# Table fetches, square sums and the programme of joins changed, and the gated convolution's strips set among attention's heads

## The chip, the cores and the metric

The kernel runs on one core of a Trainium2 chip. The metric is the device time of one execution in microseconds (us). The core has five engines that each run their own list of instructions in order and wait for one another at semaphores: TensorE (PE, matmuls), VectorE (DVE), ScalarE (ACT), GpSimd (POOL) and SyncE (SP, which here only starts transfers). Results of matmuls go to eight banks of PSUM.

## The reference

A trunk of two layers over T = 512 tokens with D = 1024 channels, all in float32. Each sub-layer is `x + rms_norm(f(rms_norm(x)))`. Layer 0 runs a gated short convolution and latent attention side by side; layer 1 a Conformer convolution; both end with a squared-ReLU MLP of 4096 hidden channels.

```python
def parallel_conv_mla(h, ...):
    proj = h @ w_in                       # 2208 columns
    gate_b, gate_c, xs, q_lat, kv_lat, k_rope = jnp.split(proj, cuts, axis=-1)
    y_a = gate_b * depthwise_conv(gate_c * xs, sc_kernel)      # width 3, 512 channels
    q = rms_norm(q_lat, q_norm) @ w_uq    # 8 heads of 64 + 32 (rope)
    kv = rms_norm(kv_lat, kv_norm) @ w_ukv
    ...
    y_b = block_attention(q_full, k_full, v)
    return jnp.concatenate([y_a, y_b], axis=-1) @ w_out

def conformer_conv(h, ...):
    a, g = jnp.split(h @ w_pw1 + b_pw1, 2, axis=-1)
    u = depthwise_conv(a * sigmoid(g), w_dw) + b_dw            # width 31
    return silu(layer_norm(u, ln_g, ln_b)) @ w_pw2 + b_pw2

def squared_relu_mlp(h, w1, w2):
    return jnp.square(jax.nn.relu(h @ w1)) @ w2
```

## The kernel before

Channels lie on the 128 partitions, tokens on the free axis; a tensor of 1024 channels is eight tiles of 128x512. Each operand of a matmul is split into a high and a low part, and a product is three matmuls: high by high, high by low, low by high (`mm`, L247 to L249). Weights come in strips of 128 output channels (128x1024 numbers): SP starts the transfer into a raw tile (L223), ACT copies it rounded into a high part (`whi`, L224), POOL subtracts for the low part (`wlo`, L225). There are two raw tiles (more in later phases) and eight slots each of `whi` and `wlo`. A whole strip against 512 tokens is 24 matmuls, against half the tokens 24 of half the length.

The order of the instructions on each engine is set by the framework's list scheduler, except in the programmes M0 to M3, where M2's vector instructions stand as written. The work in order:

- Phase m0. `split_x` loads each of eight x tiles, scales it (L572) and splits it; the rms-norm's factor R0 is not known yet, so it is applied to the results. ACT squares each tile (L359), DVE adds the squares (L334), PE sums over the channels (L369), a short chain on DVE makes the reciprocal root (L395 to L427), PE spreads it over the partitions (L434) and ACT copies it to R0 (L596).
- Five latent strips (`latent`, L604 multiplies by R0), the strip of the rope key, and the rope tables (L617 to L648: a transfer of the positions on ACT's queue, a chain on DVE and one Sin on ACT). The rope key's strip is multiplied by the table times R0 (L656).
- The gated convolution: `for i in range(4)`, three strips each (`win[6]` to `win[17]`), evicted by DVE with R0 (L672, L678, L695), the three taps on DVE, the two products on POOL (L679, L696). Its accumulators alternate between the PSUM banks S (three) and pj (two).
- V (four blocks, L715 to L727), then eight heads in the order of the table ATT: 'P' projects K (for two heads) and Q through pj banks, 'A' and 'B' attend for one half of the tokens: scores in S, maximum, exponential on ACT (L760), scaling (L763), transposes (L766) and the product with V in bank o.
- M0: the output projection wout for half A, `join` for A, wout for B. M2: a list of steps: up and down strips of the MLP's four groups, pw1 (two strips, Sigmoid, L801, product u, L805, and the start of a width-31 convolution on DVE), norm (LayerNorm and Silu, L863), pw2. A `join` or `norm` is a chain: sums of squares over channels, reciprocal root, spread, scale and split. While such a chain waits, `hold` and `pace` pull the steps that stand behind it in the list, if they belong to the other half of the tokens; what is pulled ends at the next step of the chain's own half. M3 is the last group.

A dummy activation is put ahead of a Sigmoid or Silu so that ACT loads its function table early: `nc.scalar.activation(warm[0], warm[0], AF.Sigmoid)` in `join` (L502) and the same with Silu in `layer_norm` (L848). `warm` is one tile, set once.

Of the kernel before, what the change touches and what calls it, by code (L numbers as in the profile page):

```python
# [132 lines left out]
def trunk(ctx: ExitStack, tc: tile.TileContext, a, out: bass.AP):  # L133
# [435 lines left out]
    def split_x(j):  # L569
        load_x(xs[j], j)  # L570
        t, (hi, lo) = scratch(T), (h.t[:, :T] for h in hs[j])
        nc.vector.tensor_scalar(out=t, in0=xs[j].t, scalar1=col(gains(0, 0) + j), scalar2=None, op0=ALU.mult)  # L572
# [96 lines left out]
    for i in range(4):  # L669
        accc = linear(strip(a["win"][6 + 3 * i]), hs)  # L670
        tcg = tmp("pr")[:, :T]
        nc.vector.tensor_tensor(out=tcg, in0=accc, in1=R0, op=ALU.mult)  # L672
        accx = linear(strip(a["win"][7 + 3 * i]), hs)
        cx = tmp("pr")
        nc.gpsimd.memset(cx[:, 0:1], 0.0)
        nc.gpsimd.memset(cx[:, T + 1 : T + 2], 0.0)
        tx = tmp("tq")
        nc.vector.tensor_tensor(out=tx, in0=accx, in1=R0, op=ALU.mult)  # L678
        nc.gpsimd.tensor_tensor(out=cx[:, 1 : T + 1], in0=tx, in1=tcg, op=ALU.mult)  # L679
        v = tmp("pr")[:, :T]  # L680
        nc.vector.tensor_scalar(
            out=v, in0=cx[:, 0:T], scalar1=col(V_SC + i * 3), scalar2=None, op0=ALU.mult
        )
        for k in (1, 2):
            nc.vector.scalar_tensor_tensor(
                out=v,
                in0=cx[:, k : k + T],
                scalar=col(V_SC + i * 3 + k),
                in1=v,
                op0=ALU.mult,  # L690
                op1=ALU.add,
            )
        accb = linear(strip(a["win"][8 + 3 * i]), hs)
        tb = tmp("pr")[:, :T]
        nc.vector.tensor_tensor(out=tb, in0=accb, in1=R0, op=ALU.mult)  # L695
        nc.gpsimd.tensor_tensor(out=v, in0=v, in1=tb, op=ALU.mult)  # L696
# [141 lines left out]
    def layer_norm(seg):  # L838
# [9 lines left out]
        nc.scalar.activation(warm[0], warm[0], AF.Silu)  # L848
# [300 lines left out]
```

## Time and profile before

| | us |
|---|---|
| median of three runs | 1176.1 (1175.84 to 1176.19) |
| the profiled execution | 1176.2 |
| its span | 1174.4 |
| PE busy | 1135.2 (97%) |
| POOL busy | 846.6 (72%) |
| ACT busy | 667.8 (57%) |
| DVE busy | 648.6 (55%) |

The span is the time from the first to the last instruction in the trace; 1.8 us lie around it. The mean granted clock of PE is 0.991. In a row of the profile stand start and duration, engine, line, operation, the tile written, the tiles read, the shape, and, in brackets, how long the engine was idle before it and on what it waited. S, pj, o and mi are PSUM banks, h the split input, hid the MLP's hidden tiles, ycat temporaries of phase m0, m and x the two streams of activations, pr the probabilities and pt their transposes, s small columns.

### The profile page before, as it was taken

Reading aid. Unit: us, or ns where it says so; the run is one execution under the profiler, and the core shown is the slowest. Engines: PE = TensorE matmul, PEld = TensorE weight load, DVE = VectorE, ACT = ScalarE, POOL = GpSimd, SP = SyncE. Lnnn points to the kernel's source line nnn. Section 1 sums busy time; section 2 is a strip of 40 time slices with the busy share of each in tenths; the row PEclk is TensorE's granted clock in tenths of the full one; section 3 lists DMA queues with packets and bytes.
Section 4 is the critical chain, followed back from the end, with each engine's and each line's share of the span. In section 5 each row is a group of like instructions: output and inputs, shape, how many; then the busy total and the mean of one; then the engine's idle time right before and its main releaser. Section 6 shows DMA issues by size and latency. Waiting matters only on the chain.

```text
span 1174.4 us, 22870 instructions
## 1 busy us (share of the span) xinstructions
PE 1135.2 (97%) x8850; PEld 1096.5 (93%) x8850; DVE 648.6 (55%) x1701; ACT 667.8 (57%) x1220; POOL 846.6 (72%) x409
## 2 busy tenths in 40 slices
PE   6999989999999999999999999999999999999995
PEld 4888879999999999899999999899999999999995
DVE  5652699554522124599965265699975272322123
ACT  7521667556845457545566678546467685545352
POOL 4664553148988888688886878698888877877681
PEclk9999999999999999999999999999999999999998
DMA  6421332037655555455554655455555555653431
GB/s 193 157 89 36 97 108 72 1 105 240 200 180 190 188 173 189 135 201 184 179 195 147 200 178 184 139 200 197 197 177 183 179 172 170 197 180 127 156 130 39
DMA packets 55405, 184.00 MB, mean 157 GB/s; under 512 B 6400, under 2 KB 10880, under 8 KB 55296
## 3 DMA queue, kind: packets, MB, share of 16 engines
q1 hardware_dynamic: 54720, 181.86, 46.8%
q8 instruction: 69, 1.13, 0.4%
q10 hardware_dynamic: 576, 0.68, 0.2%
q14 instruction: 40, 0.33, 0.1%
HBM read 180.42 MB, written 2.10 MB: 155 GB/s over the span
## 4 chain that ended last, share of the span: by engine, by line
PE 86%; ACT 4%; DVE 4%; POOL 2%; DMA 2%; issue 1%; POOLq 0%; ACTq 0%; DVEq 0%
PE S L247 22%; PE S L248 21%; PE S L249 21%; PE pj L247 6%; PE pj L248 6%; PE pj L249 6%; POOL wlo L225 2%; DMA raw<-in_w 1%; ACT whi L224 1%; DVE pr L763 1%; PE mi L369 1%; PE mi L434 1%; PE mi L766 1%; PE o L248 1%; DVE s L757 1%
## 5 line engine op out<-in xcount | busy, mean ns | idle before, releaser
L225 POOL TENSOR_TENSOR wlo<-raw,whi 128x1024 fp32r<-128x1024 f32 (+2 forms) x347 | 803.5, 2330 | 258.2 <-ACT whi L224 249.6
L224 ACT ACTIVATE whi<-raw 128x1024 fp32r<-128x1024 f32 (+2 forms) x347 | 355.9, 1031 | 378.0 <-PE S L248 173.1
L247 PE MATMUL S<-h,whi 128*128 128x256 f32 (+3 forms) x1208 | 347.3, 290 | 5.5 <-ACT h L231 3.7
L248 PE MATMUL S<-h,whi 128*128 128x256 f32 (+3 forms) x1208 | 348.4, 289 | 0.0
L249 PE MATMUL S<-h,wlo 128*128 128x256 f32 (+3 forms) x1208 | 348.3, 289 | 0.0
L247 PEld LDWEIGHTS S<-h,whi 128*128 128x128 f32 x1208 | 227.8, 190 | 10.8 <-ACT h L231 4.3
L247 PE MATMUL S<-hid,whi 128*128 128x256 f32 (+2 forms) x824 | 230.3, 282 | 2.3 <-DVE acc L334 1.8
L249 PEld LDWEIGHTS S<-h,wlo 128*128 128x128 f32 x1208 | 229.1, 190 | 3.5
L248 PEld LDWEIGHTS S<-h,whi 128*128 128x128 f32 x1208 | 228.9, 190 | 3.5 <-issue 0.2
L248 PE MATMUL S<-hid,whi 128*128 128x256 f32 (+2 forms) x824 | 230.9, 281 | 0.0
L249 PE MATMUL S<-hid,wlo 128*128 128x256 f32 (+2 forms) x824 | 230.4, 281 | 0.0
L828 DVE SCALAR_TENSOR_TENSOR pj<-u,taps,pj 128x240 f32<-128x240 f32 (+1 forms) x464 | 190.9, 483 | 1.0
L247 PEld LDWEIGHTS S<-hid,whi 128*128 128x128 f32 x824 | 154.8, 189 | 3.3 <-DVE acc L334 2.2
L249 PEld LDWEIGHTS S<-hid,wlo 128*128 128x128 f32 x824 | 155.6, 189 | 0.0
L248 PEld LDWEIGHTS S<-hid,whi 128*128 128x128 f32 x824 | 155.5, 189 | 0.1
L247 PE MATMUL pj<-h,whi 128*128 128x272 f32 (+3 forms) x344 | 105.8, 308 | 11.9 <-ACT h L231 10.2
L248 PE MATMUL pj<-h,whi 128*128 128x272 f32 (+3 forms) x344 | 105.1, 306 | 0.5 <-DVE h L234 0.5
L249 PE MATMUL pj<-h,wlo 128*128 128x272 f32 (+3 forms) x344 | 104.5, 304 | 0.0
L247 PEld LDWEIGHTS pj<-h,whi 128*128 128x128 f32 x344 | 64.9, 189 | 15.7 <-ACT h L231 11.0
L237 DVE TENSOR_TENSOR hid<-S,hid 128x256 fp32r<-128x256 f32 (+2 forms) x102 | 42.8, 420 | 54.3 <-ACT hid L231 54.0
L248 PEld LDWEIGHTS pj<-h,whi 128*128 128x128 f32 x344 | 65.0, 189 | 4.2 <-DVE h L234 1.8
L249 PEld LDWEIGHTS pj<-h,wlo 128*128 128x128 f32 x344 | 65.0, 189 | 2.6
(250 smaller groups left out, 1661.7 us busy)
## 6 DMA issues: line engine op xcount, KB each, us to landing
raw<-in_w SPq DMA_DIRECT2D x256, 512.0 KB, 3.3
raw<-in_pw SPq DMA_DIRECT2D x48, 512.0 KB, 3.4
raw<-in_win SPq DMA_DIRECT2D x16, 512.0 KB, 3.3
x<-in_xT SPq DMA_DIRECT2D x16, 256.0 KB, 4.6
raw<-in_wout SPq DMA_DIRECT2D x8, 512.0 KB, 3.3
raw<-in_wq SPq DMA_DIRECT2D x8, 192.0 KB, 2.3
...
```

The lines of the kernel that those rows point to most:

```text
L224: nc.scalar.activation(h, r, AF.Copy)
L225: nc.gpsimd.tensor_tensor(out=lo[:, c0:c1], in0=r, in1=h.bitcast(F32), op=ALU.subtract)
L237: eng.tensor_tensor(out=lo, in0=src, in1=hi.bitcast(F32), op=ALU.subtract)
L247: nc.tensor.matmul(acc, sh, mh, start=i == 0, stop=False)
L248: nc.tensor.matmul(acc, sh, ml, start=False, stop=False)
L249: nc.tensor.matmul(acc, sl, mh, start=False, stop=i == n - 1)
L369: nc.tensor.matmul(s[:, b : b + 1], q[:, sl.start - self.seg.lo : sl.stop - self.seg.lo], one, start=i == 0, stop=i == len(self.parts) - 1,)
L434: nc.tensor.matmul(o[:, sl], r[:, b : b + 1].to_broadcast([bw, P]), ident[:bw, :bw], start=True, stop=True,)
L757: nc.vector.reduce_max(out=mx, in_=S, axis=AX.X)
L763: eng.tensor_scalar(out=pr_, in0=pr_, scalar1=sm, scalar2=None, op0=ALU.mult)
L766: nc.tensor.transpose(tp[:, kb * P : (kb + 1) * P], pr_[:, kb * P : (kb + 1) * P], ident)
L828: nc.vector.scalar_tensor_tensor(out=dst, in0=src, scalar=wk, in1=acc, op0=ALU.mult, op1=ALU.add)
```

## The change

Five edits.

1. `split_x` squares x four tiles later (LAG); the last four squares come after all x tiles.
2. The dummy activations read a tile of the moment instead of `warm`: the Sigmoid's the squares' sum, the Silu's the negative mean. Each writes a small new tile.
3. In M2 the first group of pw1's steps is preceded by four down strips instead of two, for A and for B.
4. The gated convolution is a generator of pieces: three per group, and each piece computes one strip in a pj bank. The three pieces of the first group run where the loop stood; the other nine are taken one after every second entry of ATT. Temporaries come from ycat (16 tiles); the halo columns and their zeroing are gone, the outer taps work on 511 columns.
5. The tables TE and TO, V, Q and K's table lie in halves of weight-strip slots (`wtiles`) instead of slots of h, since h is read until the last gated strip.

```diff
-M2 = [... ('down', 'B', 0, 0, 0, 2), ('pw1', 'A', 0, 8), ('down', 'B', 0, 0, 2, 8), ... ('down', 'A', 1, 0, 0, 2), ('pw1', 'B', 0, 8), ('down', 'A', 1, 0, 2, 8), ...]
+M2 = [... ('down', 'B', 0, 0, 0, 4), ('pw1', 'A', 0, 8), ('down', 'B', 0, 0, 4, 8), ... ('down', 'A', 1, 0, 0, 4), ('pw1', 'B', 0, 8), ('down', 'A', 1, 0, 4, 8), ...]
+LAG = 4
+    def table():
+        return new(sp, "table", 2, 1)
...
         bc = rstds(ssq)
-        nc.scalar.activation(warm[0], warm[0], AF.Sigmoid)
+        nc.scalar.activation(table(), ssq.parts[0][:, :1], AF.Sigmoid)
...
         split((hi, lo), t, nc.vector, late=late)
-        s0.square(xs[j].t)
+        if j >= LAG:
+            s0.square(xs[j - LAG].t)
...
+    for j in range(NC - LAG, NC):
+        s0.square(xs[j].t)
+        settle()
...
-    for i in range(4):
-        accc = linear(strip(a["win"][6 + 3 * i]), hs)
...
+    def gated(i):
+        def part(n):
+            acc = linear(strip(a["win"][6 + 3 * i + n]), hs, acc=ps("pj"))
+            t = tmp("ycat")
+            nc.vector.tensor_tensor(out=t, in0=acc, in1=R0, op=ALU.mult)
+            return t
+
+        tcg = part(0)
+        yield
+        tx, cx, v = part(1), tmp("ycat"), tmp("ycat")
+        nc.gpsimd.tensor_tensor(out=cx, in0=tx, in1=tcg, op=ALU.mult)
+        w = [col(V_SC + i * 3 + k) for k in range(3)]
+        nc.vector.tensor_scalar(out=v, in0=cx, scalar1=w[1], scalar2=None, op0=ALU.mult)
+        for k, dst, src in ((0, v[:, 1:T], cx[:, : T - 1]), (2, v[:, : T - 1], cx[:, 1:T])):
             nc.vector.scalar_tensor_tensor(
+                out=dst, in0=src, scalar=w[k], in1=dst, op0=ALU.mult, op1=ALU.add
             )
+        yield
+        nc.gpsimd.tensor_tensor(out=v, in0=v, in1=part(2), op=ALU.mult)
         h = ypair()
         split((h[0].t, h[1].t), v, nc.gpsimd)
         ya.append(h)
+        yield
+
+    pieces = (i for n in range(4) for i in gated(n))
+    for _ in range(3):
+        next(pieces)
...
-    TE, TO = ht(), ht()
+    def wtiles(tag, dt=F32R):
+        t = new(wp, tag, N_W, STRIP, dt)
+        return t[:, :T], t[:, T:]
+
+    TE, TO = wtiles("wlo", F32)
...
-        h = ht(F32R), ht(F32R)
-        split(h, acc, nc.vector, rkv_c[:, b : b + 1])
-        V.append(h)
-    Qs = [(ht(F32R), ht(F32R)) for _ in range(2)]
+        if b % 2 == 0:
+            pair = tuple(zip(wtiles("whi"), wtiles("wlo")))
+        split(pair[b % 2], acc, nc.vector, rkv_c[:, b : b + 1])
+        V.append(pair[b % 2])
+    Qs = list(zip(wtiles("whi"), wtiles("wlo")))
...
-            tkns[p] = ht()
+            if p % 2 == 0:
+                tkns[p], tkns[p + 1] = wtiles("whi", F32)
...
-    for h, half in ATT:
+    for n, (h, half) in enumerate(ATT):
         if half == "P":
             project(h)
         else:
             attend(h, A if half == "A" else B)
+        if n % 2:
+            next(pieces, None)
...
-        nc.scalar.activation(warm[0], warm[0], AF.Silu)
+        nc.scalar.activation(table(), mu[:, :1], AF.Silu)
```

The new lines shift those that follow: a line of the kernel before has a number 1 to 15 higher in the changed one. The lists below name a tile by its kind and a running number.

The first place is the start of ACT's list. Before, with L502 and L848 the dummy activations of `warm`, L359 the squares, L231 the high part of an x tile (h):

```order
L562 ACT_TABLE_LOAD
L562 ACTIVATE s_75<-s_75 128x1
L502 ACT_TABLE_LOAD
L502 ACTIVATE warm_2837<-warm_2837 128x1
L848 ACT_TABLE_LOAD
L848 ACTIVATE warm_2837<-warm_2837 128x1
L502 ACT_TABLE_LOAD
L502 ACTIVATE warm_2837<-warm_2837 128x1
L848 ACT_TABLE_LOAD
L848 ACTIVATE warm_2837<-warm_2837 128x1
L359 ACTIVATE ycat_107<-x_79 128x512
L224 ACTIVATE whi_110<-raw_109 128x128
```

and now, with L360 the squares and L232 the high parts:

```order
L567 ACT_TABLE_LOAD
L567 ACTIVATE s_75<-s_75 128x1
L360 ACTIVATE ycat_151<-x_79 128x512
L225 ACTIVATE whi_108<-raw_107 128x128
L232 ACTIVATE h_87<-mi_104 128x512
L225 ACTIVATE whi_108<-raw_107 128x896
L225 ACTIVATE whi_122<-raw_121 128x256 x2
L232 ACTIVATE h_89<-o_117 128x512
L225 ACTIVATE whi_122<-raw_121 128x256 x2
L232 ACTIVATE h_91<-mi_137 128x512
L232 ACTIVATE h_93<-o_142 128x512
L232 ACTIVATE h_95<-mi_147 128x512
```

Four table loads with their dummies are gone from the start, and the squares but one stand further back.

The second place lies between the latents and attention. On PE before, pj_456 is the rope key's strip, S_519 the first gated strip, pj_552 and S_593 the next two, mi_481 the sums for the latents' norm:

```order
L249 MATMUL S_519<-h_101,wlo_515 128x512
L369 MATMUL mi_481<-kst,ycat_365 128x1 x4
L247 MATMUL pj_552<-h_87,whi_547 128x512
L248 MATMUL pj_552<-h_88,whi_547 128x512
...
L249 MATMUL pj_552<-h_101,wlo_548 128x512
L247 MATMUL S_593<-h_87,whi_588 128x512
```

and now, where S_646 is the first block of V and pj_519 the first gated strip:

```order
L250 MATMUL pj_519<-h_101,wlo_515 128x512
L248 MATMUL S_646<-whi_641,m_367 128x512
L248 MATMUL S_657<-whi_641,m_367 128x512
L248 MATMUL S_666<-whi_641,m_367 128x512
L370 MATMUL mi_481<-kst,ycat_365 128x1 x4
L248 MATMUL pj_552<-h_87,whi_547 128x512
L249 MATMUL pj_552<-h_88,whi_547 128x512
L250 MATMUL pj_552<-h_87,wlo_548 128x512
```

All gated strips are in pj banks now, so that pj_552 takes the bank of pj_456, and V's matmuls begin among them. On POOL at this place before, wlo_548 belongs to the second gated strip, and one gated strip follows upon another:

```order
L225 TENSOR_TENSOR wlo_548<-raw_546,whi_547 128x1024
L225 TENSOR_TENSOR wlo_589<-raw_587,whi_588 128x1024
L225 TENSOR_TENSOR wlo_627<-raw_625,whi_626 128x1024
L225 TENSOR_TENSOR wlo_660<-raw_658,whi_659 128x1024
L225 TENSOR_TENSOR wlo_701<-raw_699,whi_700 128x1024
L225 TENSOR_TENSOR wlo_739<-raw_737,whi_738 128x1024
```

and now, where L689 and L697 are the convolution's two products, wlo_642 is V's strip and L238 a low part of the convolution's result:

```order
L226 TENSOR_TENSOR wlo_548<-raw_546,whi_547 128x1024
L226 TENSOR_TENSOR wlo_587<-raw_585,whi_586 128x1024
L689 TENSOR_TENSOR ycat_579<-ycat_577,ycat_544 128x512
L697 TENSOR_TENSOR ycat_580<-ycat_580,ycat_616 128x512
L226 TENSOR_TENSOR wlo_642<-raw_640,whi_641 128x1024
L238 TENSOR_TENSOR ycat_620<-ycat_580,ycat_619 128x512
```

V's low part stands behind both products of the first group.

The third place is the join of half A at the end of layer 0 (after `('down', 'A', 0, 3, 0, 8)`), on PE. Before, S_5694 is a down strip of the other half, mi_5669 the spread of the reciprocal root, and S_5749, S_5826 and S_5851 are the first strips that read the join's h:

```order
L247 MATMUL S_5694<-hid_5258,whi_5511 128x256
L248 MATMUL S_5694<-hid_5259,whi_5511 128x256
L249 MATMUL S_5694<-hid_5258,wlo_5512 128x256
L434 MATMUL mi_5669<-kst,s_5623 128x128 x2
L247 MATMUL S_5749<-h_2181,whi_5547 128x256
L247 MATMUL S_5826<-h_2181,whi_5638 128x256
```

and now, where S_5720 is one more strip of the other half, mi_5650 the spread, and S_5795 to S_5897 the strips that read h:

```order
L248 MATMUL S_5676<-hid_5239,whi_5492 128x256
L249 MATMUL S_5676<-hid_5240,whi_5492 128x256
L250 MATMUL S_5676<-hid_5239,wlo_5493 128x256
L248 MATMUL S_5720<-hid_5225,whi_5528 128x256
...
L249 MATMUL S_5720<-hid_5240,whi_5528 128x256
L250 MATMUL S_5720<-hid_5239,wlo_5529 128x256
L435 MATMUL mi_5650<-kst,s_5604 128x128 x2
L248 MATMUL S_5795<-h_2164,whi_5619 128x256
L248 MATMUL S_5872<-h_2164,whi_5715 128x256
L248 MATMUL S_5897<-h_2164,whi_5752 128x256
```

A whole strip, S_5720, has come between the last part of the strips before and the spread.

More of the change, by code (lines that the diff above doesn't have):

```diff
@@ L35 @@
 M1 = []
-M2 = [('up', 'A', 0, 0, 0, 8), ('join', 'B', 0, 1), ('down', 'A', 0, 0, 0, 8), ('up', 'A', 0, 1, 0, 8), ('down', 'A', 0, 1, 0, 8), ('up', 'A', 0, 2, 0, 8), ('down', 'A', 0, 2, 0, 8), ('up', 'A', 0, 3, 0, 8), ('down', 'A', 0, 3, 0, 8), ('join', 'A', 0, 3), ('up', 'B', 0, 0, 0, 8), ('down', 'B', 0, 0, 0, 2), ('pw1', 'A', 0, 8), ('down', 'B', 0, 0, 2, 8), ('up', 'B', 0, 1, 0, 8), ('down', 'B', 0, 1, 0, 8), ('up', 'B', 0, 2, 0, 2), ('norm', 'A'), ('up', 'B', 0, 2, 2, 8), ('down', 'B', 0, 2, 0, 8), ('pw2', 'A', 0, 8), ('join', 'A', 1, 1), ('up', 'B', 0, 3, 0, 8), ('down', 'B', 0, 3, 0, 8), ('join', 'B', 0, 3), ('up', 'A', 1, 0, 0, 8), ('down', 'A', 1, 0, 0, 2), ('pw1', 'B', 0, 8), ('down', 'A', 1, 0, 2, 8), ('up', 'A', 1, 1, 0, 8), ('down', 'A', 1, 1, 0, 8), ('up', 'A', 1, 2, 0, 6), ('norm', 'B'), ('up', 'A', 1, 2, 6, 8), ('down', 'A', 1, 2, 0, 8), ('up', 'A', 1, 3, 0, 4), ('pw2', 'B', 0, 8), ('join', 'B', 1, 1), ('up', 'A', 1, 3, 4, 8), ('down', 'A', 1, 3, 0, 8), ('up', 'B', 1, 0, 0, 8), ('down', 'B', 1, 0, 0, 6), ('finish', 'A'), ('down', 'B', 1, 0, 6, 8), ('up', 'B', 1, 1, 0, 8), ('down', 'B', 1, 1, 0, 8), ('up', 'B', 1, 2, 0, 8), ('down', 'B', 1, 2, 0, 8)]
+M2 = [('up', 'A', 0, 0, 0, 8), ('join', 'B', 0, 1), ('down', 'A', 0, 0, 0, 8), ('up', 'A', 0, 1, 0, 8), ('down', 'A', 0, 1, 0, 8), ('up', 'A', 0, 2, 0, 8), ('down', 'A', 0, 2, 0, 8), ('up', 'A', 0, 3, 0, 8), ('down', 'A', 0, 3, 0, 8), ('join', 'A', 0, 3), ('up', 'B', 0, 0, 0, 8), ('down', 'B', 0, 0, 0, 4), ('pw1', 'A', 0, 8), ('down', 'B', 0, 0, 4, 8), ('up', 'B', 0, 1, 0, 8), ('down', 'B', 0, 1, 0, 8), ('up', 'B', 0, 2, 0, 2), ('norm', 'A'), ('up', 'B', 0, 2, 2, 8), ('down', 'B', 0, 2, 0, 8), ('pw2', 'A', 0, 8), ('join', 'A', 1, 1), ('up', 'B', 0, 3, 0, 8), ('down', 'B', 0, 3, 0, 8), ('join', 'B', 0, 3), ('up', 'A', 1, 0, 0, 8), ('down', 'A', 1, 0, 0, 4), ('pw1', 'B', 0, 8), ('down', 'A', 1, 0, 4, 8), ('up', 'A', 1, 1, 0, 8), ('down', 'A', 1, 1, 0, 8), ('up', 'A', 1, 2, 0, 6), ('norm', 'B'), ('up', 'A', 1, 2, 6, 8), ('down', 'A', 1, 2, 0, 8), ('up', 'A', 1, 3, 0, 4), ('pw2', 'B', 0, 8), ('join', 'B', 1, 1), ('up', 'A', 1, 3, 4, 8), ('down', 'A', 1, 3, 0, 8), ('up', 'B', 1, 0, 0, 8), ('down', 'B', 1, 0, 0, 6), ('finish', 'A'), ('down', 'B', 1, 0, 6, 8), ('up', 'B', 1, 1, 0, 8), ('down', 'B', 1, 1, 0, 8), ('up', 'B', 1, 2, 0, 8), ('down', 'B', 1, 2, 0, 8)]
@@ L668, in trunk @@
     ya = []
-    for i in range(4):
-        accc = linear(strip(a["win"][6 + 3 * i]), hs)
[L671 to L684, printed above, removed]
-            nc.vector.scalar_tensor_tensor(
[L686 to L691, printed above, removed]
-            )
[L693 to L696, printed above, removed]
+    def gated(i):
[11 more added lines that the diff above has]
+        for k, dst, src in ((0, v[:, 1:T], cx[:, : T - 1]), (2, v[:, : T - 1], cx[:, 1:T])):
+            nc.vector.scalar_tensor_tensor(
+                out=dst, in0=src, scalar=w[k], in1=dst, op0=ALU.mult, op1=ALU.add
+            )
+        yield
+        nc.gpsimd.tensor_tensor(out=v, in0=v, in1=part(2), op=ALU.mult)
         h = ypair()
@@ L878, in start @@
                 convolve(*todo.pop(0))
-    hid, sums, kept, us, lack, warm = {}, {}, {}, [], {}, []
+    hid, sums, kept, us, lack = {}, {}, {}, [], {}
     def seg_of(h, layer):
@@ L1033, in trunk @@
     us.extend(tmp("u") for _ in range(NC))
-    warm.append(new(sp, "warm", 1, 1))
-    nc.vector.memset(warm[0], 0.0)
     vs = [m.t for m in ms]
```

## The prediction

> **What bounds the kernel now.** I read the head of the page first, then a table of stretches, then the waits of TensorE (PE).
>
> ```profile
> PE 1135.2 (97%) x8850; PEld 1096.5 (93%) x8850; DVE 648.6 (55%) x1701; ACT 667.8 (57%) x1220; POOL 846.6 (72%) x409
> ```
>
> PE is busy in 97% of the span of 1174.4 us. The arithmetic on PE is the same in both kernels, so only the other 39 us can change, and the time in which PE is busy at a lower clock. Around the span lie 1.8 us (the profiled execution took 1176.2 us; the median of the runs shown is 1176.1, so what is summed against the one holds for the other). The stretches below give PE's busy time first, then weight loads, VectorE (DVE), ScalarE (ACT), GpSimd (POOL), and the granted clock:
>
> ```profile
> 10.00:20.00 10.00, 8.62 (x26) 4.91 (x25) 9.28 (x15) 9.15 (x18) 6.54 (x6) 1.00 0.61 203
> 60.00:120.00 60.00, 60.00 (x267) 48.82 (x266) 24.29 (x40) 11.79 (x18) 31.40 (x29) 1.00 0.19 59
> 140.00:150.00 10.00, 8.74 (x50) 7.21 (x49) 9.32 (x24) 9.02 (x20) 7.85 (x5) 1.00 0.45 147
> 150.00:160.00 10.00, 7.95 (x41) 6.68 (x40) 9.93 (x16) 5.78 (x12) 7.86 (x5) 0.83 0.29 92
> 170.00:180.00 10.00, 8.84 (x55) 7.24 (x54) 9.72 (x25) 8.37 (x20) 6.18 (x5) 1.00 0.20 63
> 470.00:480.00 10.00, 8.10 (x66) 7.65 (x65) 4.83 (x20) 6.32 (x14) 6.24 (x3) 1.00 0.43 147
> 480.00:490.00 10.00, 10.00 (x72) 9.96 (x73) 5.20 (x14) 3.55 (x8) 2.75 (x3) 0.83 0.32 107
> 740.00:750.00 10.00, 9.58 (x69) 9.58 (x70) 5.72 (x15) 3.07 (x9) 2.80 (x2) 0.83 0.32 107
> ```
>
> While the gated convolution runs (60 to 120) PE is full and DVE has 24.29 of 60 us of work. In attention (140 to 180) it is the other way round: DVE 9.3 to 9.9 of 10 us, PE 8.74, 7.95, 8.84. The rows of 150, 480 and 740 show a clock of 0.83. Half the clock for 3.4 of the 10 us gives that mean, and costs 1.7 us of work. The PE waits that go with it:
>
> ```profile
> PE S L247 <- ACT h L231: 3.7, 3, 1.7
> PE o L248 <- DVE s L758: 2.6, 3, 1.3
> PE mi L434 <- DVE s L420: 2.0, 2, 1.1
> PE mi L766 <- DVE pt L237: 1.8, 1, 1.8
> PE S L247 <- DVE u L805: 0.9, 1, 0.9
> PE S L247 <- ACT y L801: 0.4, 1, 0.4
> ```
>
> The joins (L434, then h L231), the Sigmoid (u L805, y L801) and attention (L758, pt L237) are the places. The start is a tenth part:
>
> ```profile
> 0.73 1.28 ACT L562 ACT_TABLE_LOAD   x1 [0.73 <-PEq L1137]
> ...
> 3.93 0.75 DVE L572 TENSOR_SCALAR mi<-x,vec 128x512 f32<-128x512 f32 x1 [3.04 <-DMA x<-in_xT]
> 4.96 3.80 SPq L208 DMA_DIRECT2D x<-in_xT  x6
> 6.79 1.28 ACT L848 ACT_TABLE_LOAD   x1
> 8.20 0.61 ACT L359 ACTIVATE ycat<-x 128x512 f32<-128x512 f32 x1
> 8.91 0.57 ACT L231 ACTIVATE h<-mi 128x512 fp32r<-128x512 f32 x1
> 9.52 0.69 DVE L234 TENSOR_TENSOR h<-mi,h 128x512 fp32r<-128x512 f32 x1 [4.83 <-ACT h L231]
> 9.54 0.79 PE L247 MATMUL pj<-h,whi 128*128 128x512 f32 x1 [9.54 <-ACT h L231]
> ```
>
> Five table loads of 1.28 us with a dummy activation each (first and last shown) hold ACT until 8.20, though DVE scaled the first x at 3.93. PE starts at 9.54, and between 10 and 20 it is idle for another 1.38 us.
>
> **The change, part by part.** Terms are after less before, in us.
>
> *Table fetches and squares.* Four of the five loads leave the start, so ACT can run the first square when x0 is there (3.93). By the rows 8.20 to 9.54, the square, the first weight piece and h take 1.34 us from ACT's start to PE's; counted from 3.93 with a little waiting for the weights that puts the first matmul near 5.5, 4 us earlier. It can't all be kept. The six later x's are issued at 4.96, and a transfer of x takes 4.6:
>
> ```profile
> x<-in_xT SPq DMA_DIRECT2D x16, 256.0 KB, 4.6
> ```
>
> They come from about 9.6 on, and DVE spends 0.75 (L572) and 0.69 (L234) on each, so the last is not split before 9.6 + 6 x 1.44 = 18.2. The squares' adds (0.69 each) now stand behind, which helps there. Before, PE's idle time up to 20 sums to 9.54 + 1.38 = 10.9; some 3.8 of it goes. Ends: -5 (all of the earlier start and the idle time after it) and -2 (PE merely waits later for x and the third strip). The other table loads move from the start to the joins' and norms' waits. Each is 1.28 and has 3 us of spreading and DVE work beside it there: nothing, as long as that chain is the longer.
>
> *Stalls ahead of attention.* Twelve gated strips filled PE between the latents and attention. Three are left there, and all use the two pj banks alone. So what they covered comes out. The rows:
>
> ```profile
> 35.11 0.58 ACT L596 ACTIVATE R<-mi 128x512 f32<-128x512 f32 x1
> 55.89 1.06 ACT L224 ACTIVATE whi<-raw 128x1024 fp32r<-128x1024 f32 x1 [1.91 <-DMA raw<-in_win]
> 56.86 0.67 ACT L634 ACTIVATE ycat<-o,kst 128x512 f32<-128x512 f32 x1
> 57.08 0.48 PE L247 MATMUL pj<-h,whi 128*128 128x512 f32 x1
> 59.02 0.68 DVE L672 TENSOR_TENSOR pr<-S,R 128x512 f32<-128x512 f32 x1
> 61.05 0.69 DVE L656 TENSOR_TENSOR ycat<-pj,ycat 128x512 f32<-128x512 f32 x1
> 71.98 1.29 POOL L696 TENSOR_TENSOR pr<-pr,pr 128x512 f32<-128x512 f32 x1 [3.98 <-DVE pr L695]
> 73.23 2.40 POOL L225 TENSOR_TENSOR wlo<-raw,whi 128x1024 fp32r<-128x1024 f32 x1
> 118.76 1.95 PE L434 MATMUL mi<-kst,s 128*128 128x128 f32 x16
> ```
>
> (a) R0: its spread now stands one strip (24 matmuls of 0.23) later on PE, and the next strip needs the bank that the first L604 empties: after the spread come 0.58 (L596) and one multiply by R0 (0.69, as L656), about 1.4 of wait with the semaphores; two weight copies (1.06 each) stand ahead of L596 on ACT now, so up to 2.6. (b) The second gated strip needs the bank of the rope key's strip (pj_456), which the multiply L656 empties, at the end of the rope chain. Before, that strip used S and only the multiply was late, at 61.05 to 61.74, with no PE wait. PE gets there at about 54.8 now (its 57.1 of before, less 3.7 from the start, plus 1.4 from a). The chain loses the weight copy ahead of its Sin (55.89, then L634 at 56.86: 1.3 with its wait) and L672 (0.68), and starts perhaps 0.4 earlier: 61.7 - 2.4 = 59.3, so 4.5 of wait. Ends: 2 (squeezed together by an emptier DVE) and 6.9 (chain where it was). (c) V's weights: their lo part stands on POOL behind the convolution's product (L696). After the last gated matmul come an eviction 0.69, the product 1.29 and the subtraction 2.40, against two spreads of 8 matmuls on PE (the last row's 16, 1.7 of its 1.95 before the next can start): 2.7. (d) The first head: K and Q must be evicted and split before the first score, and the strip that should cover this has its hi copy on ACT behind Q's:
>
> ```profile
> 130.52 0.62 ACT L231 ACTIVATE h<-tq 128x512 fp32r<-128x512 f32 x1
> ...
> 137.22 1.06 ACT L224 ACTIVATE whi<-raw 128x1024 fp32r<-128x1024 f32 x1 [2.21 <-DMA raw<-in_wout]
> ```
>
> Eviction 0.68 and Q's hi 0.62 are 1.3 before the first scores; then a whole hi copy (1.05) and the lo subtraction: 3.3 together. Ends 1 and 4. Sum of a to d 11.9; PE lost about 1.5 in the same part before, so +10.4 (ends +6 and +13).
>
> *The clock.* The dips at 156, 480 and 740 follow upon 1.8 us of idle PE (for pt) or two waits of about 1 close together (0.9 + 1.0 at the joins); 60 to 120, without idle time, has none. So b makes one (1.7), and c or d likely another: +2.7 (ends +1.7, +5). Here a rule of the Trainium skill differs. Its page "TensorE: Matmul & The Clock Gate", section "Why this matters for your kernels", asks for gaps of more than about 3 us before the rate halves. By it b alone would dip, this term would be 1.7, and the joins' dips below would not be for the change to remove. The trace speaks against it: two gaps of about 1 us were enough at 480.
>
> *Attention.* The nine other strips (24 x 0.23 = 5.5 us each, 50 together) now stand between heads. They bring DVE 9 evictions of 0.69 and three convolutions' taps (about 2 each): 12 us of work in 50 us of time. So DVE no longer bounds heads 0 to 5. Before, PE's idle time in the three stretches is 1.26 + 2.05 + 1.16 = 4.5, the dip 1.7, and small delays perhaps 2; heads 6 and 7 still run without cover, where some 1.8 stays: -6.4 (ends -3 and -9). TE, V, Q and K lie in weight slots now, which leaves three or four of eight to strips: from a slot's release to its use pass a transfer (no longer than x's 4.6), the hi copy (1.06) and the lo (2.40), 8.1 in all, against 11 us of two strips alone: hidden. Five of wout's eight strips, not all, are ready when attention ends. The other three need 2.40 on POOL each against 2 x 2.8 of PE per strip: nothing.
>
> *Joins.* Four down strips instead of two can be pulled into a join's waits. At join A one more (24 matmuls of 0.118 = 2.8) stands on PE between the column sums L369 and the spread L434; at join B 3.7 more, and 15 matmuls (1.8) behind the spread before the first h.
>
> ```profile
> 478.13 0.71 PE L434 MATMUL mi<-kst,s 128*128 128x128 f32 x4 [0.91 <-DVE s L420]
> 479.84 0.62 PE L247 MATMUL S<-h,whi 128*128 128x256 f32 x3 [1.00 <-ACT h L231]
> 629.96 1.28 ACT L863 ACT_TABLE_LOAD   x1
> 631.26 0.56 ACT L863 ACTIVATE pj<-m,vec 128x240 f32<-128x240 f32 x1
> 638.05 0.38 PE L247 MATMUL S<-h,whi 128*128 128x240 f32 x1 [1.70 <-ACT h L231]
> ```
>
> The chain on DVE ends at 478.1 in the first row, so the wait 0.91 goes, the wait 1.00 for h stays, and with one gap left the dip (1.7) goes: -2.7. Join B: waits 1.1 and 1.0 and the dip: -3.8. The Sigmoid's fetch is moved from the first glu's path: its two waits 0.9 and 0.4 go: -1.3. Norms: the Silu fetch (1.28) leaves the path between L860 and the first Silu, but strips that covered the norm have been used up earlier, and pw2 stands right behind the spread. Norm A's chain is eight Silu (0.56), each with a split on ACT, and the weight copies among them (1.05): some 10 us, and PE has 7 to 8 us of pw2's first three strips beside it (7 of 8 parts, 9 matmuls of 0.112 to 0.118 each): wait near 2.6 where 1.70 was, +0.8 (ends -1 and +2.5); norm B kept one strip: -0.8. Sum of M2 -7.8 (ends -4 and -10).
>
> *M0's join* starts 2.8 later against its first use of h: +0.3.
>
> Sum: -3.8 + 10.4 + 2.7 - 6.4 - 7.8 + 0.3 = -4.6, so 1176.2 - 4.6 = 1171.6.
>
> **Rivals.** 0.2% of the time is 2.35 us, about what a measurement of this kernel can tell from none.
>
> 1. Slower, 1179.5: pj banks in attention. Gated strips, K and Q share two pj banks, and each eviction is queued on DVE behind softmax rows (L763, reduce, lo parts). Nine strips and eight projections each then wait for a bank. For: the 4.5 us of b is the same mechanism. Against: DVE gets 50 us for 12 of work. At 0.5 us for each of the 17 the gain is 8 less; it turns slower from 0.42 each.
>
> 2. No change, 1175.7: the clock dips by a rule other than the gaps counted here, so that the three dips of before stay (+5.1) and only b makes a new one (-1.0). The rows at 480 and 740 make it unlikely by itself. The same time follows if both norms lose 2 each for want of cover, which is likelier. The Trainium skill's rule on the clock gate, above, would give this rival's time too.
>
> 3. More gain, 1164: chains before attention end early because DVE has fewer adds (b 2, d 1, no second dip: -6) and the start keeps -5.
>
> **How the numbers follow.** Forecast 0.43 (1167.5 to 1174.5), rival 1 0.19, rival 2 0.21, rival 3 0.17. Faster by over 0.2% (below 1173.8): 0.40 + 0.17 = 0.57; same: 0.03 + 0.19 = 0.22; slower: 0.19 + 0.02 = 0.21. The range 1163 to 1180 leaves out a tenth on either side; the likeliest case's own is 1167.5 to 1174.5.
>
> **What would show it.** First matmul at 5 to 6, and the last latent strip ends some 3.8 earlier; an idle PE of 3 to 6 us ahead of the second gated strip with the successor of L656 as releaser, and a clock of 0.8 there; a gap of 2 to 3 on POOL's wlo before V; PE over 9.7 of 10 us for heads 0 to 5; no wait for L420's successor at the joins and a clock of 1.00 there; waits of 2 to 3 in the norms. The prediction is wrong if the idle time ahead of attention is below 6 or above 16, if filler strips wait for DVE, or if the joins keep their dips.

## The result: slower by 0.6%

| | us |
|---|---|
| before, median of 4 runs | 1175.97 (1174.64 to 1176.19) |
| changed, median of 4 runs | 1182.32 (1182.04 to 1184.46) |
| ratio | 1.006, 95% interval 1.0043 to 1.0078 |
| span of the changed kernel's profile | 1180.2 |

Below, lines are those of the changed kernel, 1 to 15 higher than before (mm is L248 to L250, the spread L435, the column sums L370).

The head of the page of the changed kernel:

```profile
PE 1139.4 (97%) x8850; PEld 1098.0 (93%) x8850; DVE 645.5 (55%) x1696; ACT 664.7 (56%) x1221; POOL 844.6 (72%) x401
```

PE is busy for 4.2 us more than before with the same work. Some 0.8 of it is the lower clock (four half-clock windows for three, see below the table). The rest is time between matmuls that the profile still counts as busy: from 200 to 220 PE loses 4.4 us by the count of the table below, where the row shows 2.6 idle. The stretches (PE's busy time first, then PE's weight loads, DVE, ACT, POOL, the granted clock):

```profile
10.00:20.00 10.00, 10.00 (x40) 7.81 (x39) 9.10 (x15) 7.73 (x13) 6.09 (x6) 1.00 0.60 203
40.00:60.00 20.00, 14.70 (x69) 11.98 (x69) 18.12 (x38) 8.35 (x13) 0.00 (x0) 0.92 0.07 20
60.00:80.00 20.00, 17.35 (x75) 13.99 (x76) 7.94 (x21) 3.62 (x7) 6.11 (x4) 0.91 0.06 19
80.00:100.00 20.00, 17.99 (x73) 13.24 (x72) 10.10 (x18) 11.95 (x20) 7.79 (x6) 0.91 0.24 74
100.00:160.00 60.00, 60.00 (x321) 50.76 (x321) 44.70 (x92) 28.94 (x62) 27.48 (x20) 1.00 0.16 51
160.00:180.00 20.00, 18.80 (x97) 15.56 (x96) 6.45 (x12) 9.57 (x17) 16.09 (x12) 1.00 0.35 110
200.00:220.00 20.00, 17.39 (x99) 13.85 (x98) 15.98 (x30) 11.74 (x23) 16.35 (x10) 1.00 0.58 197
470.00:480.00 10.00, 9.77 (x83) 9.60 (x83) 7.62 (x22) 9.99 (x29) 8.31 (x4) 1.00 0.58 188
480.00:490.00 10.00, 10.00 (x85) 9.81 (x83) 3.29 (x16) 7.16 (x14) 6.25 (x4) 1.00 0.40 127
640.00:650.00 10.00, 8.15 (x58) 7.82 (x57) 6.69 (x26) 5.80 (x12) 6.69 (x3) 0.86 0.59 189
740.00:750.00 10.00, 10.00 (x89) 9.86 (x88) 3.27 (x16) 7.54 (x14) 6.65 (x4) 1.00 0.40 134
```

From 40 to 100 PE is idle for 5.3 + 2.7 + 2.0 of 60 us, at a clock of 0.91 or 0.92; from 100 to 160, where the gated strips stand among the heads, it is full with DVE at 75%; from 160 to 220 it waits again. At the joins (470 to 490, 740) the clock is whole now, at norm A (640) it is not. The waits of PE that bear on the argument:

```profile
PE mi L370 <- DVE ycat L656: 3.9, 1, 3.9
PE S L248 <- ACT h L232: 3.4, 3, 1.8
PE S L249 <- POOL wlo L226: 2.6, 1, 2.6
PE S L248 <- DVE u L820: 1.9, 2, 1.1
PE S L248 <- ACT whi L232: 1.8, 1, 1.8
PE S L248 <- ACT whi L225: 1.4, 1, 1.4
PE pj L248 <- DVE ycat L613: 1.4, 1, 1.4
PE pj L248 <- ACT whi L225: 1.0, 1, 1.0
```

The start of the changed kernel:

```profile
0.73 1.28 ACT L567 ACT_TABLE_LOAD   x1 [0.73 <-PEq L1149]
3.88 0.63 ACT L360 ACTIVATE ycat<-x 128x512 f32<-128x512 f32 x1 [1.65 <-DMA x<-in_xT]
4.76 0.60 ACT L232 ACTIVATE h<-mi 128x512 fp32r<-128x512 f32 x1
5.41 0.80 PE L248 MATMUL pj<-h,whi 128*128 128x512 f32 x1 [5.41 <-ACT h L232]
```

One table load is left ahead of the first square, and the first matmul starts at 5.41. The 3.9 us for L656 are the wait of step b, at the end of the rope chain:

```profile
40.35 0.60 ACT L605 ACTIVATE R<-mi 128x512 f32<-128x512 f32 x1 [0.47 <-PE mi L435]
43.51 0.38 ACTq L626 DMA_DIRECT2D ycat<-in_positions  x1
57.75 0.74 DVE L656 SCALAR_TENSOR_TENSOR ycat<-mi,kst,R 128x512 f32<-128x512 f32 x1
58.53 0.69 DVE L665 TENSOR_TENSOR ycat<-pj,ycat 128x512 f32<-128x512 f32 x1
58.55 1.86 PE L370 MATMUL mi<-kst,ycat 128*128 128x1 f32 x8 [3.88 <-DVE ycat L656]
```

L656 here is L647 of the kernel before: it makes the table times R0 and is the last to read the mi bank in which the table is built. The column sums L370, whose own operands are ready by then, wait for that bank. The second gated strip stands behind them and starts at 60.27. It needs the pj bank that the multiply L665 (L656 before) empties at 59.22, so without the sums PE would have waited 0.7 longer for the bank that the prediction names. Both banks come free at the end of the rope chain.

To compare kernels place by place I add up what PE loses: the time from a matmul's start to the next beyond its length at full clock (230 ns for 512 columns, 125 for 272, 118 for 256, 112 for 240, 110 for the small ones), and the time to the first matmul. Half-clock windows are in it: for 3.41 us PE's clock is halved, which loses 1.7 if PE has work all the time. The last column counts them ahead of attention / in attention / in M2.

| kernel | to 30 | to 130 | to 240 | to 460 | M2, to 970 | end | windows |
|---|---|---|---|---|---|---|---|
| before | 14.3 | 0.4 | 10.0 | 0.7 | 19.0 | 5.6 | 0 / 1 / 2 |
| changed | 10.1 | 16.4 | 7.5 | 0.9 | 15.3 | 5.6 | 3 / 0 / 1 |
| e1 strips back | 10.6 | 2.9 | 8.6 | -0.2 | 14.5 | 5.7 | 0 / 0 / 1 |
| e2 strips alone | 14.2 | 9.8 | 8.9 | 0.9 | 22.5 | 5.9 | 1 / 1 / 3 |
| e3 other banks | 10.2 | 9.1 | 8.9 | 0.4 | 15.3 | 5.6 | 0 / 1 / 1 |
| e4 V first | 10.6 | 7.9 | 7.4 | 0.4 | 15.3 | 6.3 | 0 / 0 / 1 |
| e5 table alone | 12.2 | 0.7 | 8.2 | -0.1 | 14.8 | 6.2 | 0 / 0 / 1 |
| e6 programme alone | 14.3 | 0.4 | 8.6 | 0.7 | 21.9 | 5.0 | 0 / 0 / 2 |
| e7 no lag, no strips | 11.3 | 0.8 | 8.3 | -0.2 | 13.1 | 6.8 | 0 / 0 / 0 |
| e8 V first, POOL relieved | 10.4 | 8.8 | 5.6 | 0.4 | 15.1 | 5.9 | 0 / 0 / 1 |
| e9 changed without lag | 12.3 | 9.9 | 7.6 | 0.4 | 14.8 | 6.2 | 2 / 0 / 1 |
| e10 V first, five ahead | 10.8 | 14.3 | 9.2 | 0.4 | 13.4 | 5.6 | 3 / 0 / 0 |
| e11 no lag, V first, five ahead | 11.6 | 7.0 | 8.2 | 0.8 | 13.4 | 6.1 | 0 / 1 / 0 |
| e12 before again | 14.2 | 0.4 | 8.7 | 0.7 | 17.5 | 5.6 | 0 / 0 / 1 |
| e13 no products on POOL | 10.6 | 7.2 | 6.0 | 0.4 | 13.6 | 5.7 | 0 / 0 / 0 |
| e14 no taps on DVE | 10.2 | 7.3 | 8.6 | 1.1 | 15.2 | 5.7 | 0 / 1 / 1 |

Changed less before: start -4.2, ahead of attention +16.0, attention -2.5, M2 -3.7, the rest +0.2: +5.8, the difference of the spans. Of it +0.8 is the clock, four windows for three: the first of the changed kernel's (56.77 to 60.18) lies half in the wait for L656 and costs 0.8, the others 1.7 each. Without windows it is -4.2, +11.8, -0.8, -2.0 and +0.2.

### The profile page after: what moved, and what is told of

Read it like the earlier page. It is cut to its first block, busy times and chain, and to the rows that moved or that the text cites. A ratio compares the mean times of both kernels' runs of the same rounds, so it can differ in the third digit from the quotient of the medians.

```text
span 1180.2 us, 22822 instructions
## 1 busy us (share of the span) xinstructions
PE 1139.4 (97%) x8850; PEld 1098.0 (93%) x8850; DVE 645.5 (55%) x1696; ACT 664.7 (56%) x1221; POOL 844.6 (72%) x401
## 5 line engine op out<-in xcount | busy, mean ns | idle before, releaser
L226 POOL TENSOR_TENSOR wlo<-raw,whi 128x1024 fp32r<-128x1024 f32 (+1 forms) x347 | 801.8, 2330 | 233.3 <-ACT whi L225 229.9
L225 ACT ACTIVATE whi<-raw 128x1024 fp32r<-128x1024 f32 (+1 forms) x347 | 355.6, 1031 | 347.8 <-PE S L249 152.4
L248 PE MATMUL S<-h,whi 128*128 128x256 f32 (+3 forms) x1160 | 325.2, 285 | 7.2 <-ACT h L232 3.4
L249 PE MATMUL S<-h,whi 128*128 128x256 f32 (+3 forms) x1160 | 329.2, 285 | 0.3 <-DVE h L494 0.2
L250 PE MATMUL S<-h,wlo 128*128 128x256 f32 (+3 forms) x1160 | 327.6, 283 | 0.0
L248 PE MATMUL S<-hid,whi 128*128 128x256 f32 (+2 forms) x824 | 230.5, 282 | 1.8 <-DVE acc L335 1.8
L250 PE MATMUL S<-hid,wlo 128*128 128x256 f32 (+2 forms) x824 | 230.2, 280 | 0.0
L248 PEld LDWEIGHTS S<-h,whi 128*128 128x128 f32 x1160 | 217.4, 189 | 10.8 <-ACT h L232 4.2
L249 PEld LDWEIGHTS S<-h,whi 128*128 128x128 f32 x1160 | 219.5, 189 | 2.4 <-DVE h L235 0.5
L250 PEld LDWEIGHTS S<-h,wlo 128*128 128x128 f32 x1160 | 219.7, 189 | 1.1
L248 PEld LDWEIGHTS S<-hid,whi 128*128 128x128 f32 x824 | 154.7, 189 | 2.4 <-DVE acc L335 2.2
L250 PEld LDWEIGHTS S<-hid,wlo 128*128 128x128 f32 x824 | 155.4, 189 | 0.0
L248 PE MATMUL pj<-h,whi 128*128 128x272 f32 (+3 forms) x392 | 127.1, 324 | 6.8 <-ACT h L232 5.4
L249 PE MATMUL pj<-h,whi 128*128 128x272 f32 (+3 forms) x392 | 126.6, 323 | 0.0
L250 PE MATMUL pj<-h,wlo 128*128 128x272 f32 (+3 forms) x392 | 125.4, 320 | 0.0
L248 PEld LDWEIGHTS pj<-h,whi 128*128 128x128 f32 x392 | 74.5, 190 | 12.4 <-ACT h L232 5.8
L250 PEld LDWEIGHTS pj<-h,wlo 128*128 128x128 f32 x392 | 74.7, 190 | 5.8 <-POOL wlo L226 0.7
L249 PEld LDWEIGHTS pj<-h,whi 128*128 128x128 f32 x392 | 74.6, 190 | 5.7 <-DVE h L235 0.9
L238 DVE TENSOR_TENSOR hid<-S,hid 128x256 fp32r<-128x256 f32 (+2 forms) x103 | 43.1, 419 | 53.8 <-ACT hid L232 53.6
```

Of the source, the lines that this page charges most:

```text
L225: nc.scalar.activation(h, r, AF.Copy)
L226: nc.gpsimd.tensor_tensor(out=lo[:, c0:c1], in0=r, in1=h.bitcast(F32), op=ALU.subtract)
L238: eng.tensor_tensor(out=lo, in0=src, in1=hi.bitcast(F32), op=ALU.subtract)
L248: nc.tensor.matmul(acc, sh, mh, start=i == 0, stop=False)
L249: nc.tensor.matmul(acc, sh, ml, start=False, stop=False)
L250: nc.tensor.matmul(acc, sl, mh, start=False, stop=i == n - 1)
```

## The experiments

Ratios are against runs of the kernel before on the same chip (medians there 1174.7 for e1 to e4, 1174.8 for e5 to e8, 1173.4 for e9 to e11). e12 to e14 are single executions; beside e13 and e14 the kernel before took 1173.06.

**e1, the strips back.** The loop of the gated convolution and the h slots as before, other edits kept.

```diff
-    pieces = (i for n in range(4) for i in gated(n))
+    for i in range(4):    # the loop of before; V, TE, TO, Q, tkns with ht()
```

> The changed kernel with the gated convolution as it was before (loop ahead of attention, h slots for V and Q); the square lag, the table fetches and the programme of joins stay changed. Theory 1 (the strips among the heads cost +15.7 ahead of attention and give back 2.3 in it; the other edits gain 4.2 at the start and 3.7 in M2): about 1168, with no idle time over 1 us between 20 and 130. Rival (the other edits cost, by cover lost at the norms or dips placed elsewhere): 1176 or more.

1168.03, ratio 0.995 (0.9932 to 0.9967). The strips and their slots cost 13 to 14 us (13 by the ratios, 14 by the medians); the other edits together gain. But the wait for R0 (1.41 at 42.3) is there without the strips, so it isn't theirs.

**e2, the strips alone.**

```diff
-    (square lag, table(), new M2)
+    (as before)
```

> The kernel before with the strips among the heads and the weight slots alone; squares, table fetches and programme as before. Theory 1: 1176.1 + 15.7 - 2.3 = 1189.5. Rival (the earlier start is what makes PE wait at R0 and the rope table, since those chains are set by transfers and not by PE): the waits ahead of attention are some 4 shorter, 1185.5.

1186.61, ratio 1.0108 (1.0086 to 1.0129), between theory and rival. Ahead of attention it loses 9.8, not 16.4: the wait for R0 and the one for the rope chain are absent, V's lo part (2.65) and the first head (1.80 and 0.83) remain. So part of the 16 needs another edit beside the strips (e9 tells which). M2, whose code is that of before, has three windows and 1.7 more of waits (1.64 and 1.12 at the Sigmoids); why those grew was not tested.

**e3, other banks** for the first group's first and third strip:

```diff
-            acc = linear(strip(...), hs, acc=ps("pj"))
+            acc = linear(strip(...), hs, acc=ps("S") if i == 0 and n != 1 else ps("pj"))
```

> The changed kernel with the first group's first and third strip in an S bank, so that no gated strip takes the bank of the rope key's strip. Theory 1 (PE waits because of the bank): the gap of 4.05 at 58.6 goes and with it the two half-clock windows of 1.7 each: 1182.3 - 7.4 = 1175. Rival (the rope chain is waited for anyhow, by K or by the sums that share its PSUM): the gap stands a little later, 1181.

1175.38, ratio 1.0009 (0.9997 to 1.0021), as theory 1 has it. The wait at L370 and the two windows behind it are gone: 16.4 to 9.1 ahead of attention. The scheduler then also puts the column sums behind nearly all of the third gated strip (64.07). So e3 takes away the wait for the mi bank along with that for the pj bank and doesn't part the two.

**e4, V's strip earlier.**

```diff
+    next(pieces)
+    wv = strip(a["wv"])
-    for _ in range(3):
+    for _ in range(2):
         next(pieces)
```

> The changed kernel with V's weight strip fetched after the first gated strip, not after the third. Theory 1: its lo part is no longer behind the convolution's products (2.8 at 78 goes) and V's 24 matmuls (5.5) cover the wait for the bank (4.05 and two windows of 1.7): 1182.3 - 10 = 1172. Rival (V's blocks fill the S banks and wait for the latents' norm, whose sums wait for the same PSUM tile): only the 2.8 goes, 1179.5.

1173.04, ratio 0.9987 (0.9977 to 0.9998). 7.9 ahead of attention: V's matmuls cover the rope chain (0.47 of the wait at L370 is left), and wlo is in time. What the first head costs stays: PE has lost 13.4 since the start at 75, and 18.2 at 95, which is 4.8.

**e5, the table fetches alone; e6, the programme alone; e7, both.** These are the kernel before with one or both edits (`table()` for `warm`; four down strips for two).

> The kernel before with the table fetches alone (no square lag, old programme, gated loop as before). Theory 1: the start earns what ACT's free time gives, 3 to 4, and nothing in M2, since the waits for u (0.8 and 1.1) stand in the changed kernel too: 1172.5. Rival (the fetch was what the first pw1 waits for): 1.3 more in M2, 1171.

> The kernel before with the four down strips ahead of pw1 alone. Theory 1: the joins' two half-clock windows (1.7 each) and the waits of about 1 for the spread go, a half-clock window at norm A may come: 1176.1 - 4.2 = 1172. Rival (the joins' gain needs the table fetch out of the way): 1175.

> Table fetches and programme, without the square lag and without the strips among the heads. Theory 1 (the lag moves the spread of R0 behind a strip, PE waits 1.6 for it and gives back what the lag gained at the start): the same as with the lag, 1168, with no wait at R0. Rival (the lag earns its part): 1170.

e5: 1168.73, ratio 0.9957 (0.9941 to 0.9973). e6: 1178.95, 1.0045 (1.003 to 1.0061). e7: 1165.67, 0.9932 (0.9912 to 0.9952). All three differ from what was expected. The table fetches alone earn 2.1 at the start, and in e5 the waits for u are gone, as the rival said. The joins' waits are the same as before in e5,

```profile
473.75 0.71 PE L435 MATMUL mi<-kst,s 128*128 128x128 f32 x4 [0.90 <-DVE s L421]
475.46 0.62 PE L248 MATMUL S<-h,whi 128*128 128x256 f32 x3 [1.00 <-ACT h L232]
```

yet the clock behind them is whole:

```profile
480.00:490.00 10.00, 10.00 (x87) 10.00 (x86) 4.61 (x11) 5.31 (x8) 6.22 (x3) 1.00 0.28 97
740.00:750.00 10.00, 10.00 (x87) 10.00 (x86) 4.81 (x10) 5.80 (x7) 6.36 (x3) 1.00 0.19 63
```

The programme alone takes the wait for the spread away and makes others longer; PE in e6 at the first Sigmoid and at norm A:

```profile
497.07 0.39 PE L248 MATMUL S<-h,whi 128*128 128x256 f32 x1 [2.21 <-DVE u L810]
640.14 0.49 PE L248 MATMUL S<-h,whi 128*128 128x240 f32 x2 [3.27 <-ACT h L232]
```

Before, these were 0.92 and 1.70. What is pulled into the join is missing as cover behind it, and with the Sigmoid's load on the path of u that costs 2.2. Without windows M2 loses 15.6 before, 13.1 in e5, 18.5 in e6 and 13.1 in e7: the table fetches gain 2.5, the programme gains nothing on top and costs 2.9 without them. e7 against e1 is the lag: without it 1165.7, with it 1168.0 (on another chip). It earns 0.7 at the start and gives back 1.7 at R0 and 0.4 more by 130, which is 1.4 of the 2.3. The rest is less than one window, and e1's profile has one at norm A. e7 is the fastest kernel of the study and faster than both its theory and its rival had it.

**e8, POOL relieved** (on e4):

```diff
-        nc.gpsimd.tensor_tensor(out=v, in0=v, in1=part(2), op=ALU.mult)
+        nc.vector.tensor_tensor(out=v, in0=v, in1=part(2), op=ALU.mult)
-        split((h[0].t, h[1].t), v, nc.gpsimd)
+        split((h[0].t, h[1].t), v, nc.vector)
```

> V's strip fetched after the first gated strip, and the gated convolution's second product and the low part of its result on DVE instead of POOL (5 us less of POOL's work in each 15 of the heads). Theory 1 (in heads 4 to 7 POOL is full, so raw tiles come free late and the output projection's strips wait for their copies): the waits at 160 and 204 to 212 shrink by 3: 1170. Rival (DVE is still the bound there): 1174 to 1176.

1172.61, ratio 0.9983 (0.9972 to 0.9994): not told apart from e4, and between theory and rival. Attention loses 5.6 for 7.4, but the first heads 0.9 more.

**e9, the changed kernel without the lag.**

```diff
-        if j >= LAG:
-            s0.square(xs[j - LAG].t)
+        s0.square(xs[j].t)
```

> The changed kernel without the square lag alone (squares as before, all other edits stay). Theory 2 (the lag puts R0's spread a strip later; the positions' transfer stands on ACT's queue behind R0's consumers, so the rope chain ends later, and that is what PE waits 4.05 for with the bank): the wait at R0 (1.6), most of the rope wait and its two half-clock windows go, some 0.8 of the start is lost: 1182.3 - 8 = 1174. Rival (PE waits because it comes 4 us earlier and in one bank, whatever the lag): only R0's 1.6 goes, 1181.

1176.77, ratio 1.0019 (1.0009 to 1.0029). In e9 R0, the positions' transfer on ACT's queue, and the end of the rope chain:

```profile
32.64 0.58 ACT L601 ACTIVATE R<-mi 128x512 f32<-128x512 f32 x1
38.83 0.38 ACTq L622 DMA_DIRECT2D ycat<-in_positions  x1
53.40 0.74 DVE L652 SCALAR_TENSOR_TENSOR ycat<-mi,kst,R 128x512 f32<-128x512 f32 x1
```

In the changed kernel they stood at 40.35, 43.51 and 57.75. Without the lag the chain ends 4.35 earlier and PE waits neither there nor for R0, though it reaches the column sums at 55.00 (54.67 in the changed kernel). Theory 2 holds in its mechanism; its 1174 is 2.8 short. It allowed 0.8 for the start, which costs 2.2 (table), and it has no window behind V's wait, where one came (72.1; the one at 85.8, behind the first head's wait, stands in the changed kernel too).

**e10, five pieces ahead** (on e4: five gated pieces before attention for three), and **e11**, the same without the lag and with the other seven pieces from the sixth entry of ATT on:

> V's strip after the first gated strip, and five gated pieces ahead of attention instead of three. Theory 1 (the first head waits for Q's split and the next strip's copies, 4.8 in all, since too little stands on PE beside it): two more strips (11 us) cover it, 1173.0 - 4 = 1169. Rival (the waits move two strips on, because the copies on ACT and POOL are queued behind Q's in any case): 1172 to 1173.

> The changed kernel without the lag, with V's strip after the first gated strip, five pieces ahead and the other seven at every second entry from the sixth. Theory: start 0.8 worse, R0's 1.7 and the first head's 4 gone, attention as with the strips (7): 1167. To beat the version without strips and lag it must be below 1165.7; I expect it isn't, since POOL stays full in heads 4 to 7.

e10: 1178.85, ratio 1.0039 (1.0026 to 1.0052). More strips ahead are no cover: the wait of the first head has moved to 99.5 (2.16), and the wait for the rope chain is back (3.53 at 62.3, with two windows). Two weight copies of the added strips (42.8 and 46.2 on ACT) now stand ahead of the positions' transfer (46.33; 44.00 in e4), and L656 starts at 61.54 instead of 58.21. The rival is right on the first head, and the kernel is slower than either theory had it. e11: 1174.61, ratio 1.0006 (0.9994 to 1.0018), 7.6 more than expected; two waits for Q's hi part (2.20 at 91.8, 1.83 at 101.2) stay. No form with strips among the heads beat e5 or e7.

**e12, the kernel before again.**

> The kernel before once more, for a second profile. Theory (a half-clock window follows where the idle time of PE within one 3.41 us window of a grid that lies anew in each execution exceeds some 2 us): the same waits at 155, 478 and 740 to 0.1 us, but half-clock windows at other ones of them than in the first profile, and a span that differs by 1.7 for each. Rival (the windows hang on the waits alone): the same three windows.

1173.42. The waits are those of the first profile (1.77 at 155.1, 0.91 and 1.00 at 476.9 and 478.6, 1.07 and 1.00 at 737.3 and 739.0), but of the three half-clock windows only the one behind 478.6 is left:

```profile
150.00:160.00 10.00, 7.95 (x47) 6.45 (x46) 9.93 (x15) 6.29 (x13) 7.80 (x5) 1.00 0.28 91
470.00:480.00 10.00, 8.09 (x61) 7.69 (x60) 5.40 (x22) 5.76 (x12) 6.26 (x4) 0.93 0.34 111
480.00:490.00 10.00, 10.00 (x79) 10.00 (x79) 3.92 (x11) 3.86 (x7) 2.88 (x2) 0.90 0.31 102
740.00:750.00 10.00, 10.00 (x87) 10.00 (x87) 4.38 (x12) 4.89 (x9) 3.02 (x2) 1.00 0.31 107
```

The span is 2.8 shorter, and two windows fewer are worth 3.4. So the profile on which the prediction rests was one of the longer executions of its kernel.

**e13 and e14, work left out in the heads** (on e4). e13 leaves out the gated convolution's two products, e14 its three taps, so neither computes the block. What is still open is which engine bounds heads 4 to 7. Three rows of POOL's list in e4, and ACT's copy of the output projection's first strip:

```profile
192.64 3.45 POOL L238 TENSOR_TENSOR m<-whi,m 64x512 fp32r<-64x512 f32 x2
201.07 2.40 POOL L226 TENSOR_TENSOR wlo<-raw,whi 128x1024 fp32r<-128x1024 f32 x1
203.31 1.06 ACT L225 ACTIVATE whi<-raw 128x1024 fp32r<-128x1024 f32 x1
205.89 2.39 POOL L226 TENSOR_TENSOR wlo<-raw,whi 128x1024 fp32r<-128x1024 f32 x1
```

By its whole list POOL is busy without a break from 190.3 to 208.3 there, and PE waits 0.9 for that copy at 204.4.

> V's strip after the first gated strip, and both POOL products of the gated convolution left out (the taps run on the gate-less x, the result is not multiplied by the third strip; DVE's work is unchanged). Between 140 and 240 PE loses 7.4 with them. Theory 1 (POOL, full in heads 4 to 7, delays weights and low parts): the loss there falls to about 3. Rival (DVE or the chain of softmax bounds these heads): 6 to 7 stays.

> V's strip after the first gated strip, and the gated convolution's three taps on DVE left out (the first product goes straight into the second; POOL's work is unchanged). Theory 1: PE's loss between 140 and 240 stays at 6 to 7.4, since DVE is not what is waited for. Rival (DVE bounds the heads): it falls to about 3.

e13: 1169.78, e14: 1174.09. The stretch 200 to 220 in e4, e13 and e14:

```profile
200.00:220.00 20.00, 17.59 (x120) 15.00 (x119) 16.97 (x38) 12.41 (x27) 14.46 (x9) 1.00 0.27 90
```

```profile
200.00:220.00 20.00, 17.78 (x131) 16.04 (x130) 15.83 (x37) 11.83 (x26) 13.17 (x8) 1.00 0.26 89
```

```profile
200.00:220.00 20.00, 17.82 (x115) 15.80 (x115) 13.55 (x37) 11.55 (x25) 11.68 (x8) 0.91 0.26 89
```

From 130 to 240 PE loses 7.4 in e4, 6.0 in e13 and 8.6 in e14, or 6.9 without its window. POOL's products account for 1.4, so e13's theory 1 (a loss of about 3) is refuted in its size; the taps account for 0.5, as e14's theory 1 has it. Neither bounds these heads by itself. In e13 the largest waits are one of 0.94 for an eviction (186) and one of 1.25 for a scaled row (206). That the rest is the length of the chain of one head is argued, not shown.

## Why the prediction was wrong, step by step

Forecast 1171.6 (1163 to 1180), measured 1182.3.

- *Start*, -3.8: measured -4.2, first matmul at 5.41 for "near 5.5". Right.
- *Stalls a to d*, +10.4: measured +11.8 without windows. The single waits: R0 1.41 (1.4), rope 3.9 (4.5), V's lo part 2.65 (2.7), the first head 1.84, for Q's hi part (3.3, which counts two steps behind it that PE didn't wait for). The sizes were near but for the first head, and all four waits came. In b PE stood first before the mi bank of the rope table; the rope key's bank, which I named, came free 0.7 later. And PE had lost 0.4 in this part before, where the sum takes off about 1.5. Whose the waits are was wrong: I put a and b down to the strips. e1 shows a without the strips, and e9 shows that b needs the lag: it moves R0 back by a strip, and with it the positions' transfer.
- *The clock*, +2.7: +4.2, three windows, the first of them half spent in a wait, for 1.6 forecast; that is within the end of +5. Which waits make windows can't be read from an order (last section). The Trainium skill's page "TensorE: Matmul & The Clock Gate", section "Why this matters for your kernels", warns of gaps over about 3 us; here a gap of 1.84 at 89.5 was enough (2.1 in its window with the small delays), so the measurement decides against it.
- *Attention*, -6.4: measured -2.5, of which 1.7 is a window. **This step failed.** The forecast "DVE no longer bounds heads 0 to 5" came true until 160 only; then 1.8 is lost from 160 to 180 and 5.5 from 180 to 220, where I had left 1.8 in all. Before, PE lost 1.6 from 180 to 220 and was all but full there:

```profile
180.00:200.00 20.00, 20.00 (x144) 18.33 (x144) 19.25 (x46) 14.77 (x33) 8.05 (x6) 1.00 0.28 101
200.00:220.00 20.00, 19.73 (x145) 17.95 (x144) 16.13 (x46) 12.29 (x31) 4.68 (x3) 1.00 0.00 1
```

Heads 4 to 7 lose what heads 0 to 3 no longer do. The strips bring POOL and ACT work too (a copy and a subtraction each, two products and a low part each group), which I priced only as latency, and the output projection's strips come at the same time. Attention still loses 7.5 where the sum left 1.8, 5.7 too much (and it lost 10.0 before, where the sum took 8.2). Of such a loss the products make 1.4 and the taps 0.5 (e13 and e14, on e4); what makes the rest stays open.

- *Joins and norms*, -7.8: measured -3.7. **This step failed too.** The two windows at the joins (-3.4) went, but one came at norm A (+1.7), and e5 and e12 show whole clocks behind unchanged waits. So a gain that depends on where the windows fall was booked as one of the edit. The 1176.2 from which the sum starts holds three windows and lies near the top of what the kernel before takes (1171.4 to 1176.8). The waits for u were to go (-1.3): they stand at 0.8 and 1.1, since the programme uses up the strips that covered them: with the table fetches alone (e5) they are gone, with the programme added (e7) they are back at 0.8 each. The spread's waits at the joins went, as said.
- *M0's join*, +0.3: +0.2.

Rival 1 (slower, 1179.5) has the measured side but not the mechanism: the wait of a pj strip for an eviction in attention is one of 0.27, not 8 in all. Rival 2 has the windows hang on something else than the waits; they hang on the waits, and on where these fall in the grid of windows (last section). The errors are +1.5 (clock), +3.9 (attention), +4.1 (M2), +1.4 (stalls), -0.4 (start) and -0.1 (M0's join): 10.4, as +5.8 against -4.6 is.
